# An unused tile of 224 bytes in front of the weight ring of a hybrid decoder layer

## The chip, the cores and the metric

The kernel runs on one core of a Trainium2 chip. The metric is the device time of one launch in microseconds (us), as the median of several runs. Instructions run on TensorE (PE: matmuls; its weight loads are listed apart as PEld), VectorE (DVE), ScalarE (ACT) and GpSimd (POOL); SyncE (SP) issues most DMAs. SBUF, the on-chip memory, is 128 partitions; a tile is a block of columns at one byte address in all of them. An address below is always the byte within a partition.

## The reference

One layer on 512 tokens of width 1024, all in fp32. Three groups of heads work side by side on one projection of the normalised input; their outputs are joined, projected and added to x; then comes a mixture of experts.

```python
h = rms_norm(x, attn_norm[l])
proj = h @ w_in[l]
q_da, k_da, v_da, rw_cols, q_mem = jnp.split(proj, [c1, c2, c3, c4], axis=-1)
...
o_da = diff_attention(q_da, k_da, v_da, positions, ...)
o_rw = rwkv7_time_mix(rw_cols, ...)
mem_n = rms_norm(mem, mem_norm[l])
o_mem = memory_attention(q_mem, mem_n, w_mem_kv[l], ...)
mixed = jnp.concatenate([o_da, o_rw.astype(o_da.dtype), o_mem], axis=-1)
x = x + mixed @ w_out[l]
xn = rms_norm(x, ffn_norm[l])
x = x + hierarchical_moe(xn, ...)
...
for e in range(N_EXPERTS):   # 16 experts, two chosen for each token
    hdn = jax.nn.silu(xt @ w_gate[e]) * (xt @ w_up[e])
    y = y + gate[:, e:e + 1].astype(xt.dtype) * (hdn @ w_down[e])
```

## The kernel before

**Products in three parts.** Each fp32 operand of a large product is split into a rounded part and the remainder, hi and lo, both in fp32r, and `mm3` (L243) makes three matmuls of it: hi×hi (L244), hi×lo (L245), lo×hi (L246). In `T.matmul(ps, a, b)` the tile `a` is loaded as weights and the tile `b` streams over them ("moving"). In the rows of the profile the names behind the arrow are `moving,weights`.

**The weight stream.** All weights come through `WeightStream`: chunks of 128×1024 fp32 (512 KB, 4096 bytes in each partition) are loaded by SP (L88) into whichever raw tile is free, split by ScalarE into `whi` (L97) and by VectorE into `wlo` (L98), used, and their tiles returned. `ring` holds two raw tiles, `raw0` and `raw1`, and four pairs `whi0`/`wlo0` to `whi3`/`wlo3`. Later, tiles that have become free serve as raw tiles too: `f1`, `f2`, `kT`, `qT`, `u1`, `u2` and others of `bigr`, `lraw` and `xhi`/`xlo` of `late`, and `eraw` of the pool `ex`.

**Stages.** First x and mem are normalised and split: `hm_h`/`hm_l` hold h, transposed (L342 to L344 are its first product), and `m_hi`/`m_lo` hold mem, in the memory of the tiles that the rows call `v_da` and `qT`. Then `projections` runs: `cols_unit` (L438, 512 columns of `hm` moving, `whi` as weights), then `proj` (L460, 256 columns of `whi` moving, `hm` or, for the memory, `m_hi`/`m_lo` as weights). The attention and the RWKV recurrence are woven in between. `out_part` (L1073 to L1075) is the output projection, with the same kinds of tile as `proj`; in a part of it the pairs `xhi`/`xlo` of `late` serve beside `whi`/`wlo`. Then 16 experts follow, each on up to 96 gathered tokens: `in_product` twice (L1364) and `down` (L1395), 24 matmuls each, with 512 columns of `whi`/`wlo` moving and 96 columns of `xh`/`xl` or `hh`/`hl` as weights; the transposes of the next expert's tokens (L1355) and of the hidden layer (L1377) stand between them.

**Where tiles lie.** Pools are laid one behind another in the order in which they are opened, each tile at the next multiple of 32 bytes: `const`, `rc`, `wk`, `ring`, `bigr`, then `biga`, and `late` in its place; `hm`, `rt` and `ex` are laid from the other end. In the program as built this gives, written as a multiple of 128 and a rest:

| tile | address before | |
|---|---|---|
| raw0 (first of `ring`) | 11,680 | 91×128+32 |
| whi0, wlo0 and all other tiles of `ring` and `bigr` | raw0 + a multiple of 4096 or 1024 | rest 32 |
| m_hi (v_da), m_lo (qT), lraw, xhi, xlo | 122,272; 77,216; ... | rest 32 |
| hm_h, hm_l | 196,576; 212,960 | rest 96 |
| xh, xl, hh, hl, eraw | 222,720; 225,792; 199,168; ... | rest 0 |

All rows of these tiles that a matmul reads start a multiple of 128 bytes further, so the rest is that of every operand.

Of the kernel before, what the change touches and what calls it, by code (L numbers as in the profile page):

```python
# [10 lines left out]
F32 = mybir.dt.float32  # L11
# [9 lines left out]
P = 128  # L21
# [130 lines left out]
def hybrid_layer_kernel(ctx, tc, x, mem, positions, cols, w_in, w_kv, w_out, wa2, g2, ffn, wr, br,  # L152
# [26 lines left out]
        return pools["ps"].tile([P, 512], F32, name="pt", bufs=2)  # L179

    ring = ctx.enter_context(tc.tile_pool(name="ring", bufs=1))
    ws = WeightStream(tc)
    wv = Weave(tc)
    for i in range(4):
# [1328 lines left out]
```

## Time and profile before

| | |
|---|---|
| median of 3 runs | 619.35 us (619.13 to 619.98) |
| the profiled execution's own time | 619.01 us |
| its span, first to last instruction | 617.3 us |
| mean granted TensorE clock | 0.993 |

The page of the profile gives the busy time of each engine and the chain of work that ended last, followed back from the last instruction. Busy time of TensorE covers overlapping matmuls, whose ends are modelled. The timeline lists single instructions with their start; the difference of the starts of two neighbouring matmuls is the time that one costs in a stream. Start times have a hundredth of a microsecond, so a spacing is taken over a run of many.

### The profile page before, as it was taken

Reading aid. Unit: us, or ns where it says so; the run is one execution under the profiler, and the core shown is the slowest. Engines: PE = TensorE matmul, PEld = TensorE weight load, DVE = VectorE, ACT = ScalarE, POOL = GpSimd, SP = SyncE. Lnnn points to the kernel's source line nnn. Section 1 sums busy time; section 2 is a strip of 40 time slices with the busy share of each in tenths; the row PEclk is TensorE's granted clock in tenths of the full one; section 3 lists DMA queues with packets and bytes.
Section 4 is the critical chain, followed back from the end, with each engine's and each line's share of the span. In section 5 each row is a group of like instructions: output and inputs, shape, how many; then the busy total and the mean of one; then the engine's idle time right before and its main releaser. Section 6 shows DMA issues by size and latency. Waiting matters only on the chain.

```text
span 617.3 us, 11297 instructions
## 1 busy us (share of the span) xinstructions
PE 599.2 (97%) x4178; PEld 484.4 (78%) x4178; DVE 500.5 (81%) x899; ACT 415.8 (67%) x635; POOL 125.5 (20%) x129
## 2 busy tenths in 40 slices
PE   7999999999999999999999999999999999999992
PEld 7968899999988777989986776777777777777771
DVE  5965976799846688666488999999999999988991
ACT  6488343544458776564337788888887988888880
POOL 3901011334400232223020111111100111410001
PEclk9999999999999999999999999999999999999997
DMA  9542243322342008896999999999999999799813
GB/s 304 179 121 69 89 137 86 104 68 70 99 91 71 1 3 294 284 339 213 341 299 343 364 345 365 361 372 369 368 353 357 368 360 364 229 378 374 331 27 55
DMA packets 77504, 144.21 MB, mean 234 GB/s; under 512 B 12833, under 2 KB 30497, under 8 KB 77441
## 3 DMA queue, kind: packets, MB, share of 16 engines
q1 hardware_dynamic: 69344, 126.59, 58.5%
q0 software_dynamic: 3760, 13.24, 9.1%
q10 hardware_dynamic: 4336, 3.57, 1.9%
q8 instruction: 35, 0.57, 0.4%
q14 instruction: 29, 0.23, 0.1%
HBM read 131.72 MB, written 11.67 MB: 232 GB/s over the span
## 4 chain that ended last, share of the span: by engine, by line
PE 90%; DVE 5%; DMA 2%; ACT 1%; issue 1%; POOL 0%; POOLq 0%; DVEq 0%; ACTq 0%
PE pp L244 18%; PE pp L246 17%; PE pp L245 17%; PE py L245 5%; PE py L246 4%; PE py L244 4%; PE pp L1073 2%; DVE wlo L98 2%; PE pp L1075 2%; PE pp L1074 2%; PE pt L995 2%; PE pp L1355 2%; PE py L1211 1%; PE pc L688 1%; PE pl L1178 1%
## 5 line engine op out<-in xcount | busy, mean ns | idle before, releaser
L246 PE MATMUL pp<-whi,xl 128*96 128x512 f32 x264 | 104.1, 395 | 0.0
L245 PE MATMUL pp<-wlo,xh 128*96 128x512 f32 x264 | 103.8, 394 | 0.0
L244 PE MATMUL pp<-whi,xh 128*96 128x512 f32 x264 | 101.2, 394 | 0.8 <-ACT xh L1342 0.8
L1403 POOL DMA_INDIRECT out<-ye,sidx x16 | 23.2, 1452 | 226.4 <-DVE gidx L1305 133.8
L244 PE MATMUL pp<-whi,hm_h 128*128 128x256 f32 x224 | 64.4, 288 | 0.0
L98 DVE TENSOR_TENSOR wlo<-raw,whi 128x1024 fp32r<-128x1024 f32 x42 | 52.3, 1253 | 13.8 <-ACT whi L97 13.4
L246 PE MATMUL pp<-whi,hm_l 128*128 128x256 f32 x224 | 63.2, 282 | 0.0
L97 ACT ACTIVATE whi<-raw 128x1024 fp32r<-128x1024 f32 x42 | 44.2, 1060 | 27.7 <-PE pp L246 19.1
L245 PE MATMUL pp<-wlo,hm_h 128*128 128x256 f32 x224 | 62.4, 278 | 0.0
L244 PEld LDWEIGHTS pp<-whi,xh 128*96 128x96 f32 x264 | 42.5, 161 | 19.6 <-ACT xh L1342 1.3
L246 PEld LDWEIGHTS pp<-whi,xl 128*96 128x96 f32 x264 | 42.6, 161 | 18.4
L245 PEld LDWEIGHTS pp<-wlo,xh 128*96 128x96 f32 x264 | 42.5, 161 | 18.2
L245 PE MATMUL py<-wlo,hh 128*96 128x512 f32 x120 | 47.9, 399 | 0.0
L246 PE MATMUL py<-whi,hl 128*96 128x512 f32 x120 | 47.0, 392 | 0.0
L244 PE MATMUL py<-whi,hh 128*96 128x512 f32 x120 | 47.0, 392 | 0.0
L98 DVE TENSOR_TENSOR wlo<-lraw,whi 128x1024 fp32r<-128x1024 f32 x36 | 42.6, 1218 | 2.7 <-ACT whi L97 2.7
L98 DVE TENSOR_TENSOR wlo<-u,whi 128x1024 fp32r<-128x1024 f32 x34 | 41.6, 1252 | 3.0 <-ACT whi L97 2.9
L244 PEld LDWEIGHTS pp<-whi,hm_h 128*128 128x128 f32 x224 | 42.1, 188 | 2.0 <-issue 0.7
L246 PEld LDWEIGHTS pp<-whi,hm_l 128*128 128x128 f32 x224 | 42.2, 188 | 0.6 <-issue 0.2
L245 PEld LDWEIGHTS pp<-wlo,hm_h 128*128 128x128 f32 x224 | 42.1, 188 | 0.4 <-issue 0.2
L97 ACT ACTIVATE whi<-lraw 128x1024 fp32r<-128x1024 f32 x36 | 37.1, 1058 | 5.1 <-PE pp L246 3.6
L97 ACT ACTIVATE whi<-u 128x1024 fp32r<-128x1024 f32 x34 | 35.0, 1056 | 3.0 <-PE pp L246 2.2
(407 smaller groups left out, 1564.9 us busy)
## 6 DMA issues: line engine op xcount, KB each, us to landing
raw<-in_w_in SPq DMA_DIRECT2D x22, 512.0 KB
lraw<-in_wg SPq DMA_DIRECT2D x12, 512.0 KB
lraw<-in_wu SPq DMA_DIRECT2D x12, 512.0 KB
lraw<-in_wd SPq DMA_DIRECT2D x12, 512.0 KB
u<-in_wd SPq DMA_DIRECT2D x12, 512.0 KB
f<-in_wg SPq DMA_DIRECT2D x11, 512.0 KB
u<-in_wu SPq DMA_DIRECT2D x11, 512.0 KB
eraw<-in_wd SPq DMA_DIRECT2D x10, 512.0 KB
```

The lines of the kernel that those rows point to most:

```text
L97: nc.scalar.activation(hi, slot, AF.Copy)
L98: nc.vector.tensor_sub(lo, slot, hi.bitcast(F32))
L244: T.matmul(ps, ah, bh, start=first, stop=False)
L245: T.matmul(ps, ah, bl, start=False, stop=False)
L246: T.matmul(ps, al, bh, start=False, stop=last)
L688: paired([lambda h=h, q=q: T.matmul(pq[q][:, h * P:(h + 1) * P], bk[sr(q), ci, h], u1[sr(q), q, ci, h], start=True, stop=True) for h in ra ...
L995: T.matmul(po[:, 0:P], aws[i % 2][:, kb * P:(kb + 1) * P], qk["v"][:, kb, h * P:(h + 1) * P], start=kb == 0, stop=kb == qb)
L1073: T.matmul(o, ah, hi[:, k % 4, :], start=k == k0 and i == lead, stop=False, skip_group_check=True)
L1074: T.matmul(o, ah, lo[:, k % 4, :], start=False, stop=False, skip_group_check=True)
L1075: T.matmul(o, al, hi[:, k % 4, :], start=False, stop=k == k1, skip_group_check=True)
L1355: T.transpose(ps[:, k * CAP:(k + 1) * CAP], xg[:, (b * 4 + k) * P:(b * 4 + k + 1) * P], ident[0:CAP, 0:CAP])
L1403: G.indirect_dma_start(out, bass.IndirectOffsetOnAxis(ap=si, axis=0), ye, None, compute_op=ALU.add)
```

## The change

A tile of 56 fp32 (224 bytes), which nothing reads or writes, is laid first in `ring`. All tiles of `ring`, `bigr` and `biga`, and those of `late`, lie 224 bytes further; `raw0` lies at 11,904 = 93×128, so that the rests of 32 in the table become 0. `hm`, `rt` and `ex` (rests 96 and 0) stay where they were. No instruction, wait or DMA is added, and none moves.

```diff
     ring = ctx.enter_context(tc.tile_pool(name="ring", bufs=1))
+    ring.tile([P, 56], F32, name="gap")
     ws = WeightStream(tc)
     wv = Weave(tc)
     for i in range(4):
```

## Rows read from the trace of the kernel before

**Rows 1.** The page: busy us, share of the span, instructions.

```profile
span 617.3 us, 11297 instructions
...
PE 599.2 (97%) x4178; PEld 484.4 (78%) x4178; DVE 500.5 (81%) x899; ACT 415.8 (67%) x635; POOL 125.5 (20%) x129
```

**Rows 2.** The chain that ended last: shares by line; start us, us, what.

```profile
by line: PE pp L244 17.6%; PE pp L246 16.7%; PE pp L245 16.5%; PE py L245 4.6%; PE py L246 4.5%; PE py L244 4.5%; PE pp L1073 2.1%; DVE wlo L98 2.0%; PE pp L1075 1.9%; PE pp L1074 1.9%; PE pt L995 1.7%; PE pp L1355 1.5%; PE py L1211 1.2%; P
...
350.99 0.66 PE pp L1355 x8
...
368.84 0.66 PE pp L1355 x8
...
386.69 0.66 PE pp L1355 x8
```

**Rows 3.** Two experts: us, busy PE, PEld, DVE, ACT, POOL, clock, DMA share, GB/s.

```profile
350.99:368.84 17.85, 17.85 (x91) 12.79 (x89) 17.12 (x26) 14.78 (x18) 2.46 (x2) 1.00 1.04 355
368.84:386.69 17.85, 17.85 (x92) 12.80 (x90) 16.98 (x26) 14.77 (x18) 2.43 (x2) 1.00 1.05 368
```

**Rows 4.** Waits of SP's queue: us in total, times, longest.

```profile
SPq L88 <- DVE wlo L98: 166.3, 93, 9.4
```

**Rows 5.** Timeline of PE, memory projection: start us, modelled us, instruction.

```profile
71.73 0.28 PE L244 MATMUL pp<-whi,v_da 128*128 128x256 f32 x1
...
74.97 0.28 PE L244 MATMUL pp<-whi,v_da 128*128 128x256 f32 x1
```

**Rows 6.** Timeline of PE, a projection of h.

```profile
150.06 0.28 PE L244 MATMUL pp<-whi,hm_h 128*128 128x256 f32 x1
...
152.10 0.28 PE L244 MATMUL pp<-whi,hm_h 128*128 128x256 f32 x1
```

**Rows 7.** Timeline of PE, two runs of the output projection.

```profile
274.70 0.28 PE L1073 MATMUL pp<-xhi,hm_h 128*128 128x256 f32 x1
...
277.41 0.28 PE L1075 MATMUL pp<-xhi,hm_l 128*128 128x256 f32 x1
...
282.69 0.28 PE L1073 MATMUL pp<-xhi,hm_h 128*128 128x256 f32 x1
...
284.39 0.28 PE L1073 MATMUL pp<-xhi,hm_h 128*128 128x256 f32 x1
```

**Rows 8.** Timeline of PE, one product of an expert.

```profile
424.27 0.40 PE L245 MATMUL pp<-wlo,xh 128*96 128x512 f32 x1
...
429.83 0.40 PE L245 MATMUL pp<-wlo,xh 128*96 128x512 f32 x1
```

**Rows 9.** Timeline of PE, the second chunk of a down product.

```profile
436.31 0.39 PE L246 MATMUL py<-whi,hl 128*96 128x512 f32 x1
...
437.67 0.40 PE L246 MATMUL py<-whi,hl 128*96 128x512 f32 x1
```

**Rows 10.** Timeline of PE, `cols_unit`.

```profile
59.52 0.39 PE L246 MATMUL pp<-hm_h,wlo 128*128 128x512 f32 x1
...
61.80 0.39 PE L244 MATMUL pp<-hm_h,whi 128*128 128x512 f32 x1
```

**Rows 11.** Groups by line and form: busy us, mean ns of one, idle before.

```profile
L98 DVE TENSOR_TENSOR wlo<-lraw,whi 128x1024 fp32r<-128x1024 f32 x36 | 42.6, 1218 | 2.7 <-ACT whi L97 2.7
...
L97 ACT ACTIVATE whi<-lraw 128x1024 fp32r<-128x1024 f32 x36 | 37.1, 1058 | 5.1 <-PE pp L246 3.6 <-PE py L246 1.0 <-DVE wlo L98 0.3
...
L98 DVE TENSOR_TENSOR wlo<-eraw,whi 128x1024 fp32r<-128x1024 f32 x25 | 29.4, 1219 | 2.4 <-ACT whi L97 2.4
...
L97 ACT ACTIVATE whi<-eraw 128x1024 fp32r<-128x1024 f32 x25 | 25.8, 1058 | 2.7 <-PE pp L246 2.2 <-PE py L246 0.3
```

**Rows 12.** The same view, `proj` of h, one line of three.

```profile
L244 PE MATMUL pp<-whi,hm_h 128*128 128x256 f32 x224 | 64.4, 288 | 0.0
```

**Rows 13.** L1073 alone, before and after 282.26: busy us, count.

```profile
180.00:282.26 102.26, 19.55 (x80) 13.55 (x81) 1.00 0.46 160
282.26:312.00 29.74, 13.74 (x48) 9.05 (x48) 1.00 0.82 291
```

## Prediction

> **What bounds the kernel now.** I read the page first [rows 1]: TensorE is busy for 97% of the span, VectorE for 81%. A busy TensorE proves little, because its matmuls overlap, so the second view is the chain that ended last [rows 2]. Three marks in it, the first transposes of three successive experts, stand at 350.99, 368.84 and 386.69: each of the 16 experts takes 17.85 us, almost to the hundredth. The busy time in those stretches [rows 3] says what sets that period: PE 17.85 of 17.85 at a granted clock of 1.00, VectorE 17.12 and 16.98, ScalarE about 14.8, and 355 to 368 GB/s of loads. The loads are not late: what SP's queue waited for longest is VectorE's split L98, that is a free tile, 93 times [rows 4]. So in the expert half time is simply the sum of the spacings between matmul starts. The shares by line [rows 2] say the same of the front half: L244 to L246 and L1073 to L1075 hold most of the chain.
>
> So the question is what sets the spacing. The duration on a row (395 ns) is a modelled end; I use differences of starts. First and last row of unbroken runs, granted clock 1.00 all the way:
> - Memory projection, `whi`/`wlo` moving, `m_hi`/`m_lo` (rows say v_da, qT) as weights, 256 columns: 71.73 to 74.97, 27 gaps, 120.0 ns [rows 5].
> - Projection of h, same moving tiles, `hm` as weights, 256 columns: 150.06 to 152.10, 18 gaps, 113.3 ns [rows 6].
> - Output projection, same kinds of tile: 274.70 to 277.41, 23 gaps, 117.8 ns; but 282.69 to 284.39, 15 gaps, 113.3 ns [rows 7].
> - Expert products (96 columns of `xh`/`xl` as weights, 512 columns moving): 424.27 to 429.83, 24 gaps, 231.7 ns [rows 8].
> - Expert down product, one chunk: 436.31 to 437.67, 6 gaps, 226.7 ns [rows 9].
> - `cols_unit`, other way round (`hm` moving, `whi` as weights), 512 columns: 59.52 to 61.80, 10 gaps, 228 ns [rows 10].
>
> Two floors show, 113.3 and 226.7 ns, each 17/16 of columns/2.4 GHz (106.7 and 213.3). What lies above, up to 6.7 ns a matmul, differs between stages whose instructions have one form. Between them only the tiles differ, that is the addresses, and what ran just before.
>
> **What the change does, part by part.** It adds no instruction, DMA or wait; the order on every engine is what it was. It adds 224 bytes in front of the ring. By the layout of the two programs raw0 begins at byte 11,680 before (91×128+32) and 11,904 after (93×128), and `ring`, `bigr`, `biga` and most of `late` move along. `hm` (32 bytes short of a multiple of 128) and `xh`, `xl`, `hh`, `hl` (multiples of 128) are laid from the other side and stay. So the change shows only in durations, in four places.
>
> 1. DMA. A load into another remainder could take another time. A faster one is worth nothing in the expert half, because SP waits for free tiles [rows 4]. Taken: 0.
>
> 2. Splits (L97, L98). The kernel holds the comparison already: `eraw` tiles lie at multiples of 128, `lraw` 32 beyond one. ScalarE took 1058 ns from either, VectorE 1219 and 1218 [rows 11]. The side they write is 32 off in both, and no row has it otherwise. But in the expert half both engines have slack (0.8 us and 3 us in 17.85), so a few ns off hide under PE; a few ns on would hide too, up to 0.8/12 = 70 ns a split. Taken: 0.
>
> 3. Expert stage, 1152 matmuls (72 an expert). The moving tile stands 32 beyond a multiple of 128 and its weights on one: 96 apart modulo 128 before, 0 apart after. The nearest row at 0 apart is the memory projection, 6.7 ns above its floor [rows 5]. There the weight load is 128 columns, here 96, so I scale: 6.7×96/128 = 5.0 ns. The products now pay 231.7−226.7 = 5.0 [rows 8]. Taken: 0. Bounds: all at the floor of [rows 9], −(768×5.0) ns and about −0.8 us for the downs (some of which pay too), −4.6 us; all at the full 6.7 ns, 768×1.7+384×4.5, +3.0 us.
>
> 4. `hm` with `whi`, 256 columns: 672 in the projections (three lines of 224) and 384 in the output projection (L1073 to L1075, 128 each) [rows 12, 13]. 64 apart before, 96 apart after. The nearest row at 96 apart is the expert product, 5.0 ns above its floor. 80 of the 128 L1073 ran before 282.26 [rows 13], which I put at the upper level (240 of the 384); 144 and the 672 stand at 113.3: 816 that can lose. At 5.0 ns that is 4.1 us. But [rows 7] show two levels at one and the same distance, so distance is not all that decides; I take half, 2.0 us. How much lies on the chain: L1073 to L1075 hold 2.1+1.9+1.9 = 5.9% of 617 us [rows 2], 36 us, while 384×116.1 ns is 44.6 us; with the 672 nearly all on it, nine tenths. Taken: +1.8 us. Bounds: 0 − 240×4.5 ns = −1.1 us, and 816×6.7+240×2.2 ns = +6.0 us.
>
> `cols_unit` (144 matmuls) and the first block (L342 to L344, 96) go from 64 to 32 apart, which no row shows: −1.3 to +5.3 ns on 144 from [rows 10] (228 between 226.7 and 233.3), −0.2 to +0.8 us; taken 0. The memory projection stays at 0 apart: 0.
>
> The Trainium skill speaks against all of 3 and 4: "SBUF — State Buffer", section "Who interferes with whom", gives TensorE two independent read ports and says that it waits for nobody, so addresses would not matter and the sum would be 0. The trace differs from that by 113.3 against 120.0 ns for one form of instruction.
>
> Sum: 0+0+0+1.8 on the profiled execution's own 619.01 us gives 620.8. That execution lies 0.34 below the median of the runs; carried to 619.35 it is **621.2 us**, slower by 0.3%.
>
> **The rivals.**
> - No change. For it speak the two levels of [rows 7]: at the same remainders of the addresses, they say that the run-in decides, and the stages could lock as they do now. 619.35 us. Against it: 120.0, 113.3 and 231.7 hold through each stage, and the pattern repeats expert by expert.
> - Faster, by the experts. If 0 apart suits a 96-column load with 512 columns streaming over it, all 1152 fall to 226.7: −4.6 us; with term 4 at its +1.8, −2.8: 616.6 us. It decides from where the product's gap falls below 229 ns: (231.7−229)×768 is 2.1 us, which outweighs term 4. For it: the down chunk of [rows 9] runs at the floor. Against: the one row at 0 apart is the worst of all.
> - Faster, by the floor itself. Every moving tile now begins 32 bytes past a multiple of 64, and both floors are one extra cycle in each 16 columns, which is 64 bytes of fp32. If the extra cycle comes of straddling, it goes: 512 columns would take near 213.3 ns. Then VectorE would bound the experts at 16.98 of 17.85 us [rows 3], 0.87×15 = −13 us: 606 us. Against: `hm` and `whi` straddle alike, so no row shows an aligned stream of that length. The Trainium skill, "TensorE: Matmul & The Clock Gate", section "Back-to-back issue gap", gives N/2.4+2.5 ns, 215.8 for 512 columns; no row here is that short, and the page doesn't say at which start. By it the experts would end in the same place, since VectorE takes over first.
> - Slower by more: term 4 at its bound, the experts at theirs: +9, 628 us; half of that, 624, is more like it.
>
> **How the numbers follow.** Chances: forecast (slower by 0.2 to 0.8%) 0.38; slower by more 0.05; no change within 0.2% 0.23; faster by the experts 0.21; faster by the floor 0.13. 0.2% (1.2 us) is about what a measurement of this kernel tells from no change; the three runs span 0.14%. So faster 0.34, same 0.23, slower 0.43. The range leaves out the floor's gain and the worst of the losses, 0.18 together: the experts' full −4.6 with term 4 at its lower bound −1.1 gives 613.6, and a little more for the small terms 613.0; up, +5.5 of the +9, 624.8. The likeliest case's own range is 620.6 to 624.
>
> **What the profile after would show.** Term 4: run like [rows 6] at 116 ns or more per gap. Term 3: the marks of [rows 2] still 17.85 apart, products near 231.7. First rival: all spacings of [rows 5 to 10] as they are. Second: marks under 17.70 apart. Third: products below 226 ns, VectorE back to back and idle time before PE. Term 2 is wrong if L98 moves by more than 10 ns; term 1 if SP's waits turn from VectorE to DMA. The forecast is wrong if the floor moves at all, or if the expert stage, with more matmuls than any other, locks differently, for 1 ns there is 1.2 us.

## Result and the profile after

The changed kernel takes 624.00 us (median of 4 runs, 623.87 to 624.17) against 619.66 (619.13 to 620.74) for the kernel before in the same runs: ratio 1.0066, 95% interval 1.0051 to 1.0081. It is slower, as forecast, by 4.3 us instead of 1.8, and inside the range. The profiled execution took 624.12 us; its span is 5.1 us longer than that of before [rows 1], at a mean granted clock of 0.994 against 0.993. All line numbers after the ring are one higher.

The page after (busy us, share of the span, instructions) has the same instructions, and TensorE is again busy for 97%:

```profile
span 622.4 us, 11297 instructions
...
PE 603.2 (97%) x4178; PEld 487.6 (78%) x4178; DVE 500.4 (80%) x899; ACT 416.1 (67%) x635; POOL 124.3 (20%) x129
```

The chain that ended last (shares by line, then start us, us, what):

```profile
by line: PE pp L245 17.5%; PE pp L247 16.8%; PE pp L246 16.5%; PE py L246 4.6%; PE py L247 4.5%; PE py L245 4.5%; PE pp L1074 2.6%; PE pp L1076 2.5%; PE pp L1075 2.4%; PE pt L996 1.6%; PE pp L1356 1.5%; PE py L1212 1.2%; PE pl L1179 1.0%; P
...
354.98 0.66 PE pp L1356 x8
...
372.85 0.66 PE pp L1356 x8
...
390.71 0.66 PE pp L1356 x8
...
612.75 1.11 POOL out L1404
```

The mark that stood at 350.99 stands at 354.98: 4.0 us are lost before the experts get into their stride. The next marks are 17.87 and 17.86 apart, 17.85 before [rows 2]. The share of the output projection (L1074 to L1076) rose from 5.9 to 7.5%. In the kernel before, the chain ended with this operation of GpSimd:

```profile
608.70 1.12 POOL out L1403
```

It starts 4.05 us later now, close to the 4.3 us of the medians; the other microsecond of the span lies behind it, where no matmul runs.

The spacings are read as before, between first and last row of the same runs of matmuls. Timeline of PE after (start us, modelled us, instruction):

```profile
60.01 0.40 PE L247 MATMUL pp<-hm_h,wlo 128*128 128x512 f32 x1
...
62.35 0.39 PE L245 MATMUL pp<-hm_h,whi 128*128 128x512 f32 x1
...
72.33 0.28 PE L245 MATMUL pp<-whi,v_da 128*128 128x256 f32 x1
...
75.57 0.28 PE L245 MATMUL pp<-whi,v_da 128*128 128x256 f32 x1
...
152.38 0.28 PE L245 MATMUL pp<-whi,hm_h 128*128 128x256 f32 x1
...
154.52 0.28 PE L245 MATMUL pp<-whi,hm_h 128*128 128x256 f32 x1
...
278.21 0.28 PE L1074 MATMUL pp<-xhi,hm_h 128*128 128x256 f32 x1
...
280.94 0.28 PE L1076 MATMUL pp<-xhi,hm_l 128*128 128x256 f32 x1
...
286.15 0.28 PE L1074 MATMUL pp<-xhi,hm_h 128*128 128x256 f32 x1
...
287.91 0.28 PE L1074 MATMUL pp<-xhi,hm_h 128*128 128x256 f32 x1
...
428.32 0.39 PE L246 MATMUL pp<-wlo,xh 128*96 128x512 f32 x1
...
433.87 0.39 PE L246 MATMUL pp<-wlo,xh 128*96 128x512 f32 x1
...
440.35 0.40 PE L247 MATMUL py<-whi,hl 128*96 128x512 f32 x1
...
441.73 0.40 PE L247 MATMUL py<-whi,hl 128*96 128x512 f32 x1
```

- `cols_unit`, 10 gaps in 2.34 us: 234 ns, 228 before [rows 10].
- Memory projection, 27 gaps in 3.24: 120.0, as before [rows 5].
- Projection of h, 18 gaps in 2.14: 118.9, 113.3 before [rows 6].
- Output projection, 23 gaps in 2.73: 118.7, and 15 in 1.76: 117.3; 117.8 and 113.3 before [rows 7]. The lower level is gone.
- Expert product, 24 gaps in 5.55: 231.3, 231.7 before [rows 8].
- Down, second chunk, 6 gaps in 1.38: 230, 226.7 before [rows 9].

Over whole stages, the mean spacing of neighbouring matmuls in the trace gives the sum. Gaps above 130 ns at 256 columns and 260 at 512, in which TensorE waited or did other work, are left out, so the counts are below those of the matmuls:

| stage | gaps | before, ns | after, ns | us |
|---|---|---|---|---|
| first block | 91 | 117.8 | 119.8 | +0.18 |
| `cols_unit` | 127 | 229.3 | 233.4 | +0.52 |
| memory projection | 88 | 119.4 | 119.3 | −0.01 |
| projections of h | 608 | 114.15 | 118.05 | +2.37 |
| output projection | 344 | 115.7 | 118.45 | +0.93 |
| expert products | 764 | 231.65 | 231.35 | −0.23 |
| expert downs | 344 | 229.5 | 231.4 | +0.65 |
| sum | | | | +4.4 |

The five stages ahead of the experts come to 4.0 us, what the mark at 354.98 shows. The experts' +0.4 is not all to be seen in the chain, where the stretch from that mark to the last GpSimd operation grew by 0.06 us.

The splits did not move, and SP still waits for free tiles. Groups by line and form (busy us, mean ns, idle before), and a row of SP's waits (us, times, longest), both after:

```profile
L98 DVE TENSOR_TENSOR wlo<-lraw,whi 128x1024 fp32r<-128x1024 f32 x36 | 42.6, 1217 | 2.8 <-ACT whi L97 2.6
...
L97 ACT ACTIVATE whi<-lraw 128x1024 fp32r<-128x1024 f32 x36 | 37.1, 1058 | 5.1 <-PE pp L247 3.6 <-PE py L247 1.0 <-DVE wlo L98 0.3
```

```profile
SPq L88 <- DVE wlo L98: 172.6, 100, 10.1
```

### The profile page after: what moved, and what is told of

Same layout as the page of the kernel before. It is cut to its first block, busy times and chain, and to the rows that moved or that the text cites. A ratio compares the mean times of both kernels' runs of the same rounds, so it can differ in the third digit from the quotient of the medians.

```text
span 622.4 us, 11297 instructions
## 1 busy us (share of the span) xinstructions
PE 603.2 (97%) x4178; PEld 487.6 (78%) x4178; DVE 500.4 (80%) x899; ACT 416.1 (67%) x635; POOL 124.3 (20%) x129
## 4 chain that ended last, share of the span: by engine, by line
PE 92%; DVE 3%; DMA 2%; ACT 1%; issue 1%; POOL 0%; POOLq 0%; ACTq 0%; DVEq 0%
PE pp L245 18%; PE pp L247 17%; PE pp L246 16%; PE py L246 5%; PE py L247 4%; PE py L245 4%; PE pp L1074 3%; PE pp L1076 2%; PE pp L1075 2%; PE pt L996 2%; PE pp L1356 1%; PE py L1212 1%; PE pl L1179 1%; PE pc L689 1%; PE pp L1378 1%; DVE wlo L98 1%
## 5 line engine op out<-in xcount | busy, mean ns | idle before, releaser
L98 DVE TENSOR_TENSOR wlo<-raw,whi 128x1024 fp32r<-128x1024 f32 x42 | 52.1, 1248 | 13.8 <-ACT whi L97 13.5
L97 ACT ACTIVATE whi<-raw 128x1024 fp32r<-128x1024 f32 x42 | 44.1, 1059 | 28.0 <-PE pp L247 20.2
L98 DVE TENSOR_TENSOR wlo<-lraw,whi 128x1024 fp32r<-128x1024 f32 x36 | 42.6, 1217 | 2.8 <-ACT whi L97 2.6
L98 DVE TENSOR_TENSOR wlo<-u,whi 128x1024 fp32r<-128x1024 f32 x34 | 41.6, 1250 | 3.0 <-ACT whi L97 2.6
L97 ACT ACTIVATE whi<-lraw 128x1024 fp32r<-128x1024 f32 x36 | 37.1, 1058 | 5.1 <-PE pp L247 3.6
L97 ACT ACTIVATE whi<-u 128x1024 fp32r<-128x1024 f32 x34 | 35.1, 1056 | 3.0 <-PE pp L247 2.2
```

What stands on the lines that cost most here:

```text
L97: nc.scalar.activation(hi, slot, AF.Copy)
L98: nc.vector.tensor_sub(lo, slot, hi.bitcast(F32))
```

## Experiments

The sum says where the time went, not why. **Theory D**, the prediction's: the distance between the address from which weights are loaded and the one from which the moving tile is read, modulo 128, sets the spacing; 64 is good. **Rival A**: any shift disturbs the run-in. **Rival B**: the rest of the moving tile alone decides (32 good, 0 bad). No experiment adds, drops or moves an instruction: the 4178 matmuls stand in one order in all traces. Each ratio is to the kernel before in the same group of runs, with its 95% interval; before was at 619.9 to 620.0. Spacings are means over whole stages, as in the table, unless a run of rows is named.

**The ring moved by 128 bytes.**

```diff
-    ring.tile([P, 56], F32, name="gap")
+    ring.tile([P, 32], F32, name="gap")
```

> The gap is 128 bytes instead of 224: everything of the ring moves, but every rest modulo 128 is that of before. Theory D (the distance between the weights' and the moving tile's address modulo 128 sets the spacing): as before, 619.4 us within 1.2, projections of h at 114.2 ns, output projection 115.7, expert products 231.7, down 229.5. Rival A (any shift of the ring changes the run-in, so that the good pattern of before was luck): near 622 to 624, projections near 118. A rest modulo 256 or 512 would show as some other value between.

Measured 623.56 us, 1.0052 (1.0035 to 1.0069). Projections of h 117.5 ns, output 117.2, `cols_unit` 233.2, downs 231.75. Every rest modulo 128 is that of before, and 619.4 us had been expected of it, so theory D as stated is wrong, and so is rival B. Timeline of PE in this kernel, the run of [rows 6], 18 gaps in 2.12 us, 117.8 ns:

```profile
151.88 0.28 PE L244 MATMUL pp<-whi,hm_h 128*128 128x256 f32 x1
...
154.00 0.28 PE L244 MATMUL pp<-whi,hm_h 128*128 128x256 f32 x1
```

**The change, with `hm` moved along.**

```diff
     h_lo = hm.tile([P, KC, S], F32R, name="hm_l")
+    hm.tile([P, 8], F32, name="hpad")
```

> The change, and hm_h and hm_l 32 bytes lower (rest 64), so that hm and whi are 64 apart again as before, but each at another rest. Theory D: projections, output projection, cols_unit and first block go back to 114.2, 115.7, 229.3 and 117.8 ns; 4.1 us of the 4.5 come back, 620 us. Rival B (the rest of the moving tile itself decides, 32 being good and 0 bad): projections stay at 118, 624 us.

Measured 620.53 us, 1.0006 (0.9992 to 1.0019): the loss is gone with the ring at the address of the change. Projections 114.9, output 115.3, `cols_unit` 229.4, first block 117.8; the experts stay as with the change, 231.35 and 231.4. So it is the distance, and neither the ring's own alignment nor loads or splits, which see the same raw tiles as after the change. The same run, 18 gaps in 2.04 us, 113.3 ns:

```profile
150.79 0.28 PE L244 MATMUL pp<-whi,hm_h 128*128 128x256 f32 x1
...
152.83 0.28 PE L244 MATMUL pp<-whi,hm_h 128*128 128x256 f32 x1
```

**The expert weights moved instead.**

```diff
-                base = ex_p.tile([P, CAP], F32, name="base")
+                base = ex_p.tile([P, CAP + 8], F32, name="base")[:, 0:CAP]
```

> The kernel before, with the pool ex (xh, xl, hh, hl, eraw) 32 bytes lower, rest 96: the expert weights are 64 apart from whi and wlo instead of 96; no other tile moves. Theory D (64 apart is good): products fall from 231.7 towards 226.7 ns, downs from 229.5 to 226.7, 768 x 5.0 + 384 x 2.8 = 4.9 us less, 614.5 us; the period of an expert falls from 17.85 to 17.55. Rival B (the moving tile's own rest decides): 619.4, period 17.85.

A miss: 620.50 us, 1.0004 (0.9992 to 1.0016). Products 231.7 as before, downs 231.7 instead of 229.5. With theory D corrected to modulo 256 a reason offers itself: `xh[:, k, :]` begins 384 bytes further for each k, so the distance modulo 256 alternates, here between 64 and 192, and shifting `ex` only shifts both. The trace does not show the two apart: the matmuls of this run's products average 231.6 ns at the k of 64 and 231.9 at those of 192.

**A gap of 32.**

```diff
-    ring.tile([P, 56], F32, name="gap")
+    ring.tile([P, 8], F32, name="gap")
```

> Gap of 32 bytes: the ring has rest 64, hm is 32 apart from it, the expert weights 64 apart (in the other direction than in the run before). Theory D: projections and output projection lose as with the change (32 apart, which no 256-column row has yet; 118 ns, +3.4 us), cols_unit and first block lose too (+0.7), experts gain 4.9: 618.6 us. Rival B has no row for rest 64; it would move projections and experts in the same direction.

Measured 624.06 us, 1.0060 (1.0038 to 1.0082). Projections 118.3, output 118.2, `cols_unit` 233.2: as expected. The time is 5.5 us above the 618.6 that had been expected, because the experts gained nothing (231.7, 231.7), as in the run before. The first block, of which a loss had been expected, got faster, 116.7 ns against 117.8.

The distances so far, `hm` less `whi` modulo 256: 64 in the kernel before and with `hm` moved along, both good; 96 (the change), 192 and 32, all bad. **Theory D2**: as D, modulo 256.

**A gap of 256, the next good one by D2.**

```diff
-    ring.tile([P, 56], F32, name="gap")
+    ring.tile([P, 64], F32, name="gap")
```

> Gap of 256 bytes: whi is 64 below hm modulo 256 as before (the distances in the runs so far: 64 was good in the kernel before and with hm moved along, 32, 96 and 192 were bad). Theory D2 (the distance counts modulo 256): back to the kernel before, 619.6 to 620.5 us, projections 114 to 115 ns, cols_unit 229.4, first block 117.8. Rival A (every shift of the ring against the rest spoils the run-in): 622.5 to 624, projections at 117.5 or more, cols_unit 233.

Measured 619.88 us, 1.0002 (0.9992 to 1.0011). Projections 114.9, output 114.5, `cols_unit` 229.3, first block 117.8, downs 229.5. The ring moved further than in the change, and nothing was lost: rival A falls as well. The same run, 18 gaps in 2.04 us:

```profile
150.66 0.28 PE L244 MATMUL pp<-whi,hm_h 128*128 128x256 f32 x1
...
152.70 0.28 PE L244 MATMUL pp<-whi,hm_h 128*128 128x256 f32 x1
```

**A gap of 192: as far apart as can be.**

```diff
-    ring.tile([P, 56], F32, name="gap")
+    ring.tile([P, 48], F32, name="gap")
```

> Gap of 192 bytes: hm and whi are 128 apart modulo 256, the farthest that there is. If the two streams of TensorE hinder each other where they are near (modulo 256), this is the best distance: projections 113.3, cols_unit 227, 618 us. If 64 is a value of its own, projections 117 to 118.5 and cols_unit 233, 623 to 624 us. Experts as in all runs, 231.7.

Measured 623.31 us, 1.0058 (1.0044 to 1.0072). Projections 118.7, output 118.55, `cols_unit` 232.3; the experts 230.8 and 231.0, where 231.7 had been expected. Far is not good; for the projections 64 is a value of its own.

**One distance for all expert matmuls.** Blocks of `xh`, `xl`, `hh`, `hl` 512 bytes apart instead of 384, two output tiles instead of three to make room, and `ex` lowered by 32 (the pad of the third experiment):

```diff
-        xh = ex_p.tile([P, KC, CAP], F32R, name="xh", bufs=XB)
+        xh = ex_p.tile([P, KC, P], F32R, name="xh", bufs=XB)[:, :, 0:CAP]
...
-        ye = ex_p.tile([CAP, D], F32, name="ye", bufs=3)
+        ye = ex_p.tile([CAP, D], F32, name="ye", bufs=2)
```

> The kernel before, with expert weights laid at 512 bytes from one block of 96 columns to the next instead of 384 (so the distance to whi and wlo is one value for all k instead of four), two output tiles ye instead of three to make room, and the pool ex 32 bytes lower: weights minus moving tile is 64 modulo 256 throughout. Theory D2: products and downs fall towards 226.7 ns, up to 4.9 us less, 615 us, if 64 is good for 96 columns as well; a period of 17.55. Rival (the experts' spacing has nothing to do with addresses): 231.7 and 229.5 to 231.7, 620 us.

Measured 618.38 us, 0.9978 (0.9969 to 0.9987), faster than both kernels, by 1.5 us of the 4.9 that had been hoped for. Products 229.4 and downs 229.6 ns, in a steady pattern of four (in the trace 226, 229, 232, 226), not at the floor. Four matmuls are no multiple of the three of `mm3`, so the pattern does not belong to one of these operands or another. The marks in the chain are 17.66 and 17.68 apart:

```profile
351.13 0.66 PE pp L1355 x8
...
368.79 0.66 PE pp L1355 x8
...
386.47 0.66 PE pp L1355 x8
```

**The same at 192,** `ex` 128 bytes lower (a pad of 40 floats in place of 8).

> The same with the pool ex another 128 bytes lower: weights minus moving tile is 192 modulo 256 throughout, the value that cols_unit (512 columns moving, weights of 128) has in the kernel before, where it runs at 229.3 ns. Theory D2: 512-column matmuls at 229 or less here, 616 us, if not in the run before. Rival: no difference between this run and the last.

Measured 622.19 us, 1.0042 (1.0029 to 1.0056). Products 233.3, downs 233.4, again a pattern of four (229, 236, 237, 231); the marks are 18.00 and 18.02 apart. The expectation that a value good for `cols_unit` is good here was wrong: which distance is good differs with the form of the matmul. But addresses alone move an expert from 17.68 to 18.0 us. The mean of both runs' products, (229.4+233.3)/2 = 231.4, is within 0.4 ns of the 231.7 of the third experiment, which alternates between the two distances; that its matmuls take the two times in turn is not shown, as said there.

```profile
351.29 0.66 PE pp L1355 x8
...
369.29 0.66 PE pp L1355 x8
...
387.31 0.66 PE pp L1355 x8
```

**The same at 224 and at 128** (pads of 32 and 56 floats).

> As the pitch-512 kernel at 64, with weights minus moving tile 224 modulo 256 throughout. In the kernel before, one chunk of the down product (224 modulo 256 as well) ran six matmuls in a row at 226.7 ns, and with the gap of 128 bytes a chunk at the same value ran at 232. Theory D2 with that value good: all 1152 at 226.7, 0.99 x 4.9 us under the kernel before, 615 us, period 17.55. If the value is good only behind a certain run-in: between 229 and 233, 618 to 622.

Measured 618.63 us, 0.9980 (0.9971 to 0.9989), with runs from 617.31 to 619.77. The mean of the products is 229.6 ns, but the trace has two levels, 226.7 and 233.3, at one and the same set of addresses; at the lower every gap is 226 or 227 ns, at the upper they run from 230 to 236. The marks show it:

```profile
350.69 0.66 PE pp L1355 x8
...
368.25 0.66 PE pp L1355 x8
...
386.26 0.66 PE pp L1355 x8
...
403.82 0.66 PE pp L1355 x8
...
421.38 0.66 PE pp L1355 x8
...
439.39 0.66 PE pp L1355 x8
```

The periods are 17.56, 18.01, 17.56, 17.56 and 18.01 us. Timeline of PE in the fourth and in the fifth of these experts: 6 gaps in 1.36 us and 9 in 2.10, 226.7 and 233.3 ns:

```profile
405.69 0.39 PE L245 MATMUL pp<-wlo,xh 128*96 128x512 f32 x1
...
407.05 0.39 PE L245 MATMUL pp<-wlo,xh 128*96 128x512 f32 x1
...
423.26 0.39 PE L245 MATMUL pp<-wlo,xh 128*96 128x512 f32 x1
...
425.36 0.40 PE L245 MATMUL pp<-wlo,xh 128*96 128x512 f32 x1
```

The 615 us would have needed all experts at the floor.

> The same at 128 modulo 256, the farthest distance. In the runs with four distances the chunks at 0 and 128 ran at 231 to 232 ns. Theory D2: one steady pattern again, its mean not to be had from the runs so far, in the range of 229.4 (at 64) to 233.4 (at 192). If farthest were best, below 229.4 and under 618 us; if 64 is the only good value, 231 to 233.4, 620 to 622 us.

Measured 619.76 us, 1.0001 (0.9992 to 1.0010); products 231.2, downs 231.4, between 64 and 192, as expected of a distance that is not special. With the same two tiles `ye` this kernel takes as long as the one before, so the gain at 64 does not come from the missing third tile.

**The memory projection at 64.**

```diff
+    ring.tile([P, 16], F32, name="gap")
     bigr = ctx.enter_context(tc.tile_pool(name="bigr", bufs=1))
...
     late = ctx.enter_context(tc.tile_pool(name="late", bufs=1, reuse_waits="tile"))
+    late.tile([P, 48], F32, name="lpad")
```

> As the pitch-512 kernel at 64, and a gap of 64 bytes behind the ring with one of 192 in front of late's tiles, so that m_hi and m_lo come to lie 64 bytes above whi modulo 256 (0 in every run so far), while xhi and xlo keep their distance to hm. The memory projection has been at 119.2 to 119.4 ns in every run. Theory D2: its 96 matmuls go to 114 to 115 ns as those of h, 0.4 to 0.5 us less than the pitch-512 kernel at 64, 617.9 us. Rival (that stage is slow for another reason, its place in the program): 119.4 ns, no change.

Measured 618.09 us, 0.9974 (0.9963 to 0.9984), the lowest median of all, though its interval holds the ratio 0.9978 of the kernel at 64 without it. The stage went from 119.4 to 117.8 ns only: 27 gaps in 3.18 us. 117.8 is the upper of the two levels of [rows 7], here kept from end to end. The distance moved the stage, but not to the level that was expected, though `m_hi` and `whi` now have the rests modulo 256 that `hm` and `whi` have in the kernel before: a good distance allows the floor and does not ensure it.

```profile
71.86 0.28 PE L244 MATMUL pp<-whi,v_da 128*128 128x256 f32 x1
...
75.04 0.28 PE L244 MATMUL pp<-whi,v_da 128*128 128x256 f32 x1
```

**Multiples of 128 again, 128 bytes lower.**

```diff
-    ring.tile([P, 56], F32, name="gap")
+    ring.tile([P, 24], F32, name="gap")
```

> Gap of 96 bytes: every tile of the ring lies at a multiple of 128 as with the change, 128 bytes lower (raw0 at 11,776, a multiple of 256), so that hm is 224 above whi modulo 256 instead of 96; the expert weights keep 0 and 128. If only the rest modulo 128 counted, all spacings would be those of the change and the time 624.0. Theory D2: a value of its own, since 224 was not yet had for the projections; of the values had for them (0: 119.4, 32: 118.3, 64: 114.1 to 114.9, 96: 118.1, 128: 118.7, 192: 117.5) only 64 was good, so between 114 and 119 ns and 620 to 624 us; the experts as with the change, 231.3 and 231.4.

Measured 622.59 us, 1.0041 (1.0027 to 1.0054). Projections 116.9, output 117.2, `cols_unit` 233.0, products 231.8 and downs 230.1, where 231.3 and 231.4 had been expected: by every rest modulo 128 the kernel after the change, by time and spacings another one.

The two forms that the change hurt most, by distance (`hm` less `whi`, modulo 256):

| distance | projections of h, ns | `cols_unit`, ns |
|---|---|---|
| 32 | 118.3 | 233.2 |
| 64 (before, and 8 experiments) | 114.1 to 114.9 | 229.3 to 229.4 |
| 96 (the change) | 118.05 | 233.4 |
| 128 | 118.7 | 232.3 |
| 192 | 117.5 | 233.2 |
| 224 | 116.9 | 233.0 |

At 0 no run had the projections of h; the memory projection, of the same form, is at 119.3 to 119.5 there. 160 was not tried. The first block, with `hm` moving and 256 columns, has its own order: 115.9 ns at 192, 116.7 at 32, 117.8 at 64, 118.3 at 224, 119.4 at 128 and 119.8 at 96.

## Why the prediction held, and where its reasons failed

- **Terms 1 and 2 (loads, splits): right.** L98 from `lraw` takes 1217 ns after, 1218 before [rows 11]; L97 1058 both times. SP still waits for free tiles, 172.6 us in 100 waits, 166.3 in 93 before [rows 4].
- **Term 3 (experts, taken 0): right to +0.4 us,** −0.23 from the products and +0.65 from the downs, well inside −4.6 to +3.0. The period moved from 17.85 to 17.86 or 17.87. But "96 apart to 0 apart" was not what happened: with blocks 384 bytes apart there are two distances modulo 256, before 96 and 224, after 0 and 128, and the means of the products, over both, hardly differ. The good chunk of [rows 9] (224) was one of the two.
- **Term 4 (projections, taken +1.8): right in sign, place and kind, too small.** It measured 2.37 + 0.93 = 3.3 us. The step that was mis-sized is "I take half": the two levels of [rows 7] were read as a doubt about distance, but at every distance other than 64 that was run the projections lose 2.7 to 4.5 ns against before on the mean of the stage. Without the halving the prediction's own working gives 4.1×0.9 = 3.7. That this comes so near is in part luck: the price of 5.0 ns was taken from a row of another form at a distance counted with the wrong modulus, and measured 3.9 and 2.7; and the 240 put at the upper level throughout were not all there, since runs of the output projection that start at 244.82 and 247.09 in the trace of before stand at 113.7.
- **`cols_unit` and first block, taken 0: they lost 0.70 us,** near the upper bound of +0.8. With term 4 at its measure this makes the 4.4 of the table.
- **The reason itself was wrong in one number.** Distances were counted modulo 128, from stages whose distances differ modulo 128 as well as modulo 256. The gap of 128 bytes, which keeps all of these, costs 3.6 us; the gap of 256 costs nothing.
- **Slower by more**: the 624 that this rival called more like it is what was measured, inside the forecast's own class of 0.2 to 0.8%; but it came from the projections and `cols_unit`, with only 0.4 of the 3.0 us that the rival's bound gave the experts. **No change**: the spacings of [rows 6] and [rows 10] moved; what spoke for it, two levels at one set of addresses, is real. **Faster by the experts**: the 0 apart of the change (0 and 128 modulo 256) gives 231.35 ns, but the idea that expert weights can be laid better was sound (618.4 us at 64). **Faster by the floor**: after the change the moving tiles `whi` and `wlo` start at multiples of 128, with the gap of 96 bytes at multiples of 256, and no steady run is below 113.3 or 226.7 ns. With `hm` moved along, `whi` starts at a multiple of 128 and the run sits on 113.3 as before, so that floor does not come from straddling. The Trainium skill's formula for an isolated matmul ("TensorE: Matmul & The Clock Gate", section "Back-to-back issue gap") gives 215.8 ns for 512 columns, which was seen in no run here as a steady spacing.

What TensorE reads decides, then, not what the other engines do. In the trace after, the projections of h take 117.8 ns where a split of ScalarE or VectorE runs beside the matmuls (176 gaps) and 118.2 where none does (432); in the trace before it is 114.1 and 114.2. The Trainium skill, "SBUF — State Buffer", section "Who interferes with whom", gives TensorE two independent read ports and contention to no one but VectorE and GpSimd; by it none of the gaps would have cost anything. The trace disagrees: 114.15 against 118.05 ns for one form of matmul, by the distance of its two operands.

Open: that weight load and moving stream collide is a reading that fits, since their distance matters and not the address of either, but no run separated the two streams, and it is not shown. What puts a run of matmuls on one or the other of two levels at one distance, and why the good distance is 64 for one form and 192 for another (`whi` loaded while `hm` moves), was not found.

## What to carry to other kernels

Where TensorE runs back to back, look at the spacing of matmul starts by stage, and compare it with the lowest spacing of the same form anywhere in the trace; a few ns there were worth up to 4.4 us here, where TensorE is busy for 97% of the span. A tile moved for alignment moves against all tiles that stay: ask for the distance modulo 256 between weights and moving tile, not for the rest of one of them, and try a pad in steps of 32 bytes. Give the blocks of a weight tile a pitch that keeps this distance the same for all of them, and measure: a pitch of 512 bytes at the right offset gained 0.2% here, at the wrong one it lost 0.4%.

## What was unexpected of the hardware

- The spacing depends on the distance of the two operands modulo 256 bytes: moving the ring by 128 bytes costs 3.6 us, by 256 nothing.
- At one set of addresses there can be two steady levels: 113.3 and 117.8 ns at 256 columns, 226.7 and 233.3 at 512. An unbroken run settles on one and keeps it, the next may take the other: the output projection before has runs at both [rows 7], while in the run at 224 an expert stays at one. Experts of one run took 17.56 or 18.01 us.
- With the expert weights at 192 throughout, the spacings repeat in a fixed pattern of four (229, 236, 237, 231 ns) and never settle at the floor.
